# Held rotary swaps, earlier weight loads, and a last output tile in narrower pieces in a hybrid attention layer

## The chip, the cores and the metric

The kernel runs on one core of a Trainium2 chip. The metric is the time of one execution on the device in microseconds (us), taken as the median over runs. The engines are PE (matmul; its weight loads are listed as PEld), DVE (vector), ACT (activation and copies), POOL (general) and SP, which here only issues DMAs. Every engine works through its own instructions in the order in which the program lists them, and waits where an operand isn't ready.

## The reference

One decoder layer on x of 2048 rows by 1024 columns. Two groups of attention heads share one input projection; each branch is gated, and both go through one output projection, a root-mean-square norm and a gated residual:

```python
h = rms_norm(x, g_pre) * (1 + scale) + shift              # scale, shift, gate from silu(c) @ w_ada + b_ada
qa, ka, va, fa, za, qb, kb, vb, zb = split(h @ w_in)
oa = forgetting_attention(qa, ka, va, fa + b_fgate)       # FoX: 8 heads of 64, causal, with a cumulative log-forget bias
oa = oa * silu(za)
qb, kb = rope(qb, positions), rope(kb, positions)         # [x1*cos - x2*sin, x2*cos + x1*sin], halves of 32 columns
ob = sliding_window_sink_attention(qb, kb, vb, sinks)     # 8 query heads, 2 key/value heads, window 128, a sink per head
ob = ob * silu(zb)
y = concatenate([oa, ob]) @ w_out
x + gate * rms_norm(y, g_post)
```

The arithmetic is in float32; the kernel splits float32 operands into a high and a low float16 part and makes three products of them.

## The kernel before

The program is one order written by hand. Time on PE is cut into units (a few matmuls each, the list `punits`); `tick()` advances a list of delayed steps, and `after(n, f)` puts step `f` on that list for the n-th tick from now. So each engine's order is set by where a step's tick falls. `events` holds, for a unit's number, the steps that stand ahead of that unit.

The stages are: start and first projections (to about 155 us), the sliding-window stage (to 416), the FoX heads 0 to 6 (to 926), head 7 with the loading and splitting of `w_out` (to 1016), sixteen output tiles of 128 rows (to 1169), and the end.

In the sliding-window stage 32 objects of class `Pair` run in turn, each for two query blocks of 128 and two heads, and between their parts PE does projection units. A pair's steps are: `scores` (PE, L852); `maxima` (DVE, L866, L869); `exps` (ACT, four at L877); in `split` the `high` half, a float16 copy on ACT (L894) and a DMA transpose on SP's queue (L895), and the `low` half, a subtraction on DVE (L899), a second transpose (L900) and then `load_now()`; and, two pairs later, `pv` (PE, L915), which needs both transposes (`ptb`), with `out_` on DVE (L921, tile `on`). Four ticks make up one pair's turn.

Two other chains run through this stage in the same engines' orders.

- The rotation of queries, `evac_rope`. ACT copies the projected columns from PSUM to `qf` (L717); four DMAs on SP's queue write them with their 32-row blocks swapped to `qs` (L719); DVE multiplies the PSUM columns by the cosine into `qc` (L722); POOL multiplies `qs` by the sine (L732); DVE adds (L733); ACT copies the sum to float16, `stb` (L734); DVE makes its low part (L726). The pairs' scores read both parts. The steps after the copy are timed from the start of the chain, at 5, 6, 7 and 8 ticks plus `turn_lag`.
- The weights of each projection: `w_load` (a DMA into `wr_...`, queued until the next `load_now()` while `banded` is set), `w_max` (DVE, L224), a round trip through DRAM on POOL's queue, `w_scale`, then `w_high` (ACT, L267) and `w_low` (DVE, L273) into `wh_...`. `leads` in `add` says how many units ahead of its projection each step stands; for the load that is 46.

In head 7 the loop over steps `s` (with `r` the step within the head) loads the parts of `w_out`, makes its scale in `w_root` from sums of squares (`wss`), and loads the rows of the first two output tiles: `Out.load` fetches the attention output `o_d` and the gate `z_d`. `turn` transposes them on PE (L1436), multiplies by the gate on DVE (L1445), takes the squares on ACT (L1448), and splits the product into `oz`. `product` then makes two halves of 512 columns in 24 matmuls each (L1472); the evacuation squares on ACT (L1480) and multiplies by `gacc` on DVE (L1481); `root` takes the reciprocal root by small DVE operations, and `store` adds the residual (L1507) and writes the tile out (L1508). The last tile is stored in two halves.

Of the kernel before, what the change touches and what calls it, by code (L numbers as in the profile page):

```python
# [10 lines left out]
F32 = mybir.dt.float32  # L11
# [29 lines left out]
def hybrid_layer(  # L41
# [47 lines left out]
    def rsqrt_mean(dst, ss, n):  # L89

        v = sm(n, "rs_v")
        V.tensor_scalar(v[:], ss, 1.0 / D, EPS, op0=ALU.mult, op1=ALU.add)
# [106 lines left out]
    kaps_seen = []  # L199
    first = ("kb", "vb", "zb0", "zb1")  # L200

    queued, banded = [], [False]

    def load_now():
        todo, queued[:] = queued[:], []
        for key, pieces in todo:
            w_load(key, pieces, SP)
# [499 lines left out]
    def evac_rope(ci, finish, pool):  # L707
        cols_ = slice(ci * CH, (ci + 1) * CH)

        def evac(ps, free):  # L710
# [4 lines left out]

            def copy():
                A.activation(qf[:], ps, AF.Copy, scale=PS_SCALE)  # L717
                for r in range(4):
                    SP.dma_start(qs[32 * r:32 * r + 32, :], qf[32 * (r ^ 1):32 * (r ^ 1) + 32, :])  # L719
# [8 lines left out]

            after(1, copy)
            after(2, cos)  # L730
            d = turn_lag[0]
            after(5 + d, lambda: G.tensor_tensor(qs[:], qs[:], sinT[:, cols_], op=ALU.mult))  # L732
            after(6 + d, lambda: V.tensor_tensor(qc[:], qc[:], qs[:], op=ALU.add))  # L733
            after(7 + d, lambda: A.activation(stg[:, 0, :], qc[:], AF.Copy))  # L734
            after(8 + d, low)

        return evac

# [95 lines left out]
    class Pair:  # L834
# [44 lines left out]
        def split(self):  # L879
# [17 lines left out]
            def low():  # L897
                for p, (hi, lo) in cuts:
                    V.tensor_tensor(lo, p, hi, op=ALU.subtract)  # L899
                SP.dma_start_transpose(self.ptt[:, 1, 0:self.nt, :], part[1][:, 0:n])  # L900
# [26 lines left out]

    pkeys, punits = [], []  # L930
# [231 lines left out]
    def w_square(m):  # L1162
# [3 lines left out]
        if m < 32:  # L1166
            wsq[m] = wsp.tile([P, 2 * P], F32, tag="wsq", name="wsq")
            SP.dma_start(wsq[m][:], w_out0[m // 4 * P:(m // 4 + 1) * P, m % 4 * 2 * P:(m % 4 + 1) * 2 * P])

    def w_root():  # L1170
        wsum = sm(1, "w_mx2")
        V.tensor_reduce(wsum[:], wss[:], axis=AX.X, op=ALU.add)
        pw_ = bk[bank()][:, 0:1]
        PE.matmul(pw_, ones[:], wsum[:], start=True, stop=True)
        root_scale(wrt[:], pw_)
# [242 lines left out]
    class Out:  # L1418


        def __init__(self, t):
            self.t = t

        def load(self):
            t = self.t
            rows_ = slice(t * P, (t + 1) * P)
            self.o = Ts[0][:, t % 2, :].bitcast(F32)
            SP.dma_start(self.o, o_d[t // 4][(t % 4) * P:(t % 4 + 1) * P, :])
# [30 lines left out]
            after(lag + 2, lambda: V.scalar_tensor_tensor(lo, self.z, self.sc[:], hi, op0=ALU.mult, op1=ALU.subtract))  # L1459

        def product(self, n, k):
            cc = slice(n * CH, (n + 1) * CH)
            if k == 0:
                self.b = bank(True)
                if n == 0:
                    self.ss = sm(2, "y_ss")
                else:
                    self.x = oio["x"]()
                    SP.dma_start(self.x[:], xs[self.t * P:(self.t + 1) * P, :])
            py, b = bk[self.b][:], self.b  # L1470
            for m_, (i, j) in enumerate(((0, 0), (0, 1), (1, 0))):
                PE.matmul(py, self.hl[:, i, k, :], w_slot(8 * j + k)[:, cc],  # L1472
                          start=(k == 0 and m_ == 0), stop=(k == KT - 1 and m_ == 2))
# [3 lines left out]
            def evac():  # L1477
                if n == 0:
                    self.y = oio["y"]()
                A.activation(oio["j"][1 + n], py, AF.Square, accum_out=self.ss[:, n:n + 1])  # L1480
                V.tensor_tensor(self.y[:, cc], py, gacc[:, cc], op=ALU.mult)  # L1481
                release(b)

            after(1, evac)
            if n == 1:
                last = self.t == NB - 1
                after(2 if last else 4, self.root)
                after(2 if last else 7, self.store)

        def root(self):  # L1490
            ss = self.ss
            inv = sm(1, "w_sw")
            V.tensor_tensor(inv[:], self.sc[:], ysc[:], op=ALU.mult)
            V.reciprocal(inv[:], inv[:])
            V.tensor_tensor(ss[:, 0:1], ss[:, 0:1], ss[:, 1:2], op=ALU.add)
            V.tensor_scalar(ss[:, 0:1], ss[:, 0:1], inv[:], inv[:], op0=ALU.mult, op1=ALU.mult)  # L1496
            rst = sm(1, "y_rs")
            rsqrt_mean(rst, ss[:, 0:1], 1)
            V.tensor_tensor(rst[:], rst[:], inv[:], op=ALU.mult)
            self.rst = rst  # L1500

        def store(self):
            y, rst = self.y, self.rst
            parts = 2 if self.t == NB - 1 else 1
            for n in range(parts):
                cc = slice(n * D // parts, (n + 1) * D // parts)
                V.scalar_tensor_tensor(y[:, cc], y[:, cc], rst[:], self.x[:, cc], op0=ALU.mult, op1=ALU.add)  # L1507
# [5 lines left out]
    for t, n in [(0, 0), (1, 0), (0, 1), (1, 1)] + [(t, n) for t in range(2, NB) for n in range(2)]:  # L1513
        if n == 0 and t + 2 < NB:
            oloads[len(ounits)] = t + 2
        for q in range(KT):
# [16 lines left out]
    with tc.manual_schedule():  # L1533
# [29 lines left out]
        for s, stp_ in enumerate(steps):  # L1563
# [112 lines left out]
```

## Time and profile before

| what | value |
|---|---|
| three runs | 1177.09, 1177.81 and 1180.39 us; median 1177.81 |
| profiled execution | 1180.07 us, of which the span of the core's work is 1178.3 |
| mean granted clock of PE | 0.992 |
| PE busy | 1119.8 us, 95% of the span |
| DVE, ACT, POOL busy | 918.9, 679.1, 165.3 us |
| start and first projections | 0 to 155 us, PE busy 135.46 |
| sliding-window stage | 155 to 416 us, PE busy 247.21 |
| FoX heads 0 to 6 | 416 to 926 us, PE busy 502.64 |
| head 7 | 926 to 1016 us, PE busy 81.60 |
| output tiles | 1016 to 1169.4 us, PE busy 152.92 |
| end | 1169.4 to 1178.3 us, PE busy 0 |

Rows of single instructions read: start, duration, engine, line, operation, output<-inputs, partitions and columns, type, count; in brackets stands the idle time of the engine just before, and the instruction or DMA that ended it. Rows with "SPq" are DMAs on SP's queue, with the time that their issue took there. Rows of waits read: engine, instruction, what it waited for, total, times, longest. Rows of windows read: stretch, length, busy time and instructions of PE, PEld, DVE, ACT and POOL, then PE's granted clock, the share of time that DMA engines were busy, and GB/s.

### The profile page before, as it was taken

How to read it: one execution, taken by the hardware profiler on the slowest of the kernel's cores; microseconds unless marked ns; L12 is line 12 of the kernel's file. 1: busy time of each engine (PE TensorE's matmuls, PEld its weight loads, DVE VectorE, ACT ScalarE, POOL GpSimd, SP SyncE). 2: the span in 40 equal slices, each digit the busy share in tenths (PEclk: the TensorE clock that was granted, in tenths of full speed). 3: DMA queues.
4: the chain of work that ended last, by engine and by line, in shares of the span. 5: the costliest groups of instructions: out<-in, count | busy, mean ns of one | idle time of the engine just before them, and what ended most of it. 6: DMA issues, size and time to landing. Idle time of an engine off the chain costs nothing. (4 is left out here: it accounts for less than half of the span.)

```text
span 1178.3 us, 26992 instructions
## 1 busy us (share of the span) xinstructions
PE 1119.8 (95%) x10490; PEld 653.0 (55%) x10490; DVE 918.9 (78%) x2329; ACT 679.1 (58%) x1122; POOL 165.3 (14%) x302
## 2 busy tenths in 40 slices
PE   5899999999989999999999999999999989999996
PEld 1466656654459956555555555555555545555553
DVE  6776577888788747889888889978897886767665
ACT  4676445555556433676767667676676588323331
POOL 2011122233222211111111111102010000000000
PEclk9999999999999999999999999999999999999998
DMA  9645345687676832243223232213111254465652
GB/s 330 213 138 161 94 89 110 121 145 143 132 145 112 126 76 75 67 104 73 77 76 86 78 78 72 63 46 93 44 50 43 64 175 157 148 199 168 204 175 76
DMA packets 162452, 136.36 MB, mean 116 GB/s; under 512 B 95356, under 2 KB 139428, under 8 KB 162324
## 3 DMA queue, kind: packets, MB, share of 16 engines
q1 hardware_dynamic: 152532, 106.65, 35.6%
q0 software_dynamic: 9456, 27.72, 8.8%
q8 instruction: 82, 1.34, 0.5%
q14 instruction: 46, 0.38, 0.1%
q10 hardware_dynamic: 336, 0.26, 0.1%
HBM read 70.97 MB, written 25.18 MB: 82 GB/s over the span
## 5 line engine op out<-in xcount | busy, mean ns | idle before, releaser
L1313 ACT ACTIVATE p<-sta,lift,scl_qk 128x1024 f32<-128x1024 f32 (+2 forms) x160 | 172.0, 1075 | 95.7 <-PE sta L1309 89.9
L329 PE MATMUL bk<-hT,wh_qk 128*128 128x512 f16 x768 | 197.9, 378 | 0.6 <-DVE a_m L1262 0.6
L1472 PE MATMUL bk<-wohl,oz 128*128 128x512 f16 x768 | 172.4, 379 | 2.2 <-DVE oz L1459 1.0
L1324 DVE TENSOR_TENSOR pha<-p,pha 128x1024 f16<-128x1024 f32 (+2 forms) x160 | 169.7, 1061 | 0.0
L1321 ACT ACTIVATE pha<-p 128x1024 f16<-128x1024 f32 (+2 forms) x160 | 148.1, 926 | 31.6 <-POOL p L1317 26.8
L1262 DVE TENSOR_REDUCE a_m<-bk 128x1 f32<-128x512 f32 x192 | 129.4, 684 | 36.4 <-PE bk L1259 35.6
L1472 PEld LDWEIGHTS <-oz 128*128 128x128 f16 x768 | 74.4, 99 | 84.2 <-issue 1.8
L1334 PE MATMUL poa<-vt,pha 128*128 128x65 f16 x1088 | 116.5, 193 | 1.6 <-DVE ona L1343 1.6
L1337 PE MATMUL poa<-vt,pha 128*128 128x65 f16 x1088 | 116.0, 192 | 1.4 <-DVE pha L1324 1.4
L1336 PE MATMUL poa<-vt,pha 128*128 128x64 f16 x1088 | 116.3, 194 | 0.0
L1308 PE MATMUL sta<-T 128*128 128x512 f16 (+1 forms) x320 | 109.6, 347 | 6.3 <-ACT p L1313 6.3
L1259 PE MATMUL bk<-T 66*128 66x512 f16 (+2 forms) x320 | 110.5, 348 | 2.1 <-DVE a_m L1262 2.1
L1334 PEld LDWEIGHTS <-pha 128*128 128x128 f16 x1088 | 101.6, 97 | 16.3 <-DVE ona L1343 2.9
L329 PEld LDWEIGHTS <-wh_qk 128*128 128x128 f16 x768 | 70.2, 97 | 71.6 <-issue 2.9
L1336 PEld LDWEIGHTS <-pha 128*128 128x128 f16 x1088 | 101.0, 97 | 13.4
L1309 PE MATMUL sta<-T 69*128 69x512 f16 (+1 forms) x320 | 108.0, 348 | 0.0
L1337 PEld LDWEIGHTS <-pha 128*128 128x128 f16 x1088 | 100.8, 99 | 1.6 <-DVE pha L1324 1.6
L329 PE MATMUL bk<-hT,wh_za 128*128 128x512 f16 x384 | 99.9, 379 | 0.0
L347 PE MATMUL bk<-wh_va,hT 128*128 128x128 f16 x1536 | 95.9, 223 | 1.8 <-DVE wh_va L273 1.8
L347 PEld LDWEIGHTS <-hT 128*128 128x128 f16 x1536 | 90.6, 100 | 8.1 <-issue 5.5
L329 PE MATMUL bk<-hT,wh_zb 128*128 128x512 f16 x384 | 92.8, 384 | 2.2 <-DVE wh_zb L273 2.2
L1317 POOL TENSOR_SCALAR_AFFINE_SELECT p<-p 128x256 f32<-128x256 f32 x64 | 31.9, 499 | 416.3 <-ACT p L1313 411.5
(492 smaller groups left out, 1858.3 us busy)
## 6 DMA issues: line engine op xcount, KB each, us to landing
hT<-in_x_dram SPq DMA_DIRECT2D x20, 512.0 KB
wa<-in_w_ada_dram SPq DMA_DIRECT2D x16, 512.0 KB
T<-stq SPq DMA_DIRECT2D x128, 64.0 KB
T<-o_d SPq DMA_DIRECT2D x16, 512.0 KB
T<-z_d SPq DMA_DIRECT2D x16, 512.0 KB
z_d<-tz POOLq DMA_DIRECT2D x30, 256.0 KB, 2.9
out_dram<-hT SPq DMA_DIRECT2D x15, 512.0 KB
xt<-in_x_dram SPq DMA_DIRECT2D x12, 512.0 KB
```

The costliest lines, as they stand in the source:

```text
L329: PE.matmul(ps, whl[:, a, k, :], hT[ci][:, b, k, :], start=(k == 0 and n == 0), stop=(k == KT - 1 and n == 2))
L347: PE.matmul(ps[:, u * P:(u + 1) * P], hT[ci][:, a, k, u * P:(u + 1) * P], whl[:, b, k, :], start=(k == 0 and n == 0), stop=(k == KT - 1 an ...
L1259: PE.matmul(mx[:, :w], T[0:XM, 0, i * P:(i + 1) * P], T[0:XM, 2, pc * CH:pc * CH + w], start=True, stop=True)
L1262: V.tensor_reduce(m3[:, u, pc:pc + 1], mx[:, :w], axis=AX.X, op=ALU.max)
L1308: PE.matmul(self.st[:, o:o + w], T[:, 3, kb_], T[:, 1, qc], start=True, stop=False)
L1313: A.activation(self.p32[:, :self.w], self.st[:, :self.w], AF.Exp, scale=scl[f"qk{self.hd}"][:], bias=lift[:])
L1321: A.activation(self.ph[:, 0, :self.w], self.p32[:, :self.w], AF.Copy)
L1324: V.tensor_tensor(self.ph[:, 1, :self.w], self.p32[:, :self.w], self.ph[:, 0, :self.w], op=ALU.subtract)
L1334: PE.matmul(po[:, u, :], ph[:, 0, pq], vt[:, b, hd, 0:65], start=(self.first and n == 0 and u == 0), stop=False)
L1336: PE.matmul(po[:, u, 0:64], ph[:, 0, pq], vt[:, b, hd, 65:VW], start=False, stop=False)
L1337: PE.matmul(po[:, u, :], ph[:, 1, pq], vt[:, b, hd, 0:65], start=False, stop=(self.last and n == len(self.blocks) - 1))
L1472: PE.matmul(py, self.hl[:, i, k, :], w_slot(8 * j + k)[:, cc], start=(k == 0 and m_ == 0), stop=(k == KT - 1 and m_ == 2))
```

## The change

It has four parts.

1. While `banded` is set, the four swap DMAs of a rotation are put on a list, `swaps`, and issued by the next `load_now`, that is behind a pair's second transpose. The steps after them are timed from there: POOL's product 4 ticks later, DVE's add 5, ACT's copy 6, the low part 7. When swaps were issued, weight loads that are queued wait for the next pair's call.
2. The loads of weights after the first stage stand 64 units ahead of their projection (58 for `qk0`) instead of 46.
3. In head 7, the gate rows of the first two output tiles are loaded at steps 1 and 2, ahead of the attention rows at 4 and 6; every output tile loads its gate first. The last sum over `wss` for `w_root` is taken at step 134 instead of at 136.
4. The last output tile is made in pieces of 512, 384 and 128 columns, 24 matmuls each. Its factor `inv` is multiplied in at the evacuation, what can be had without the last 128 columns is computed ahead, and the second half is stored from ACT's queue.

```diff
@@ load_now, evac_rope
+    def load_now(must=True):
+        todo, swaps[:] = swaps[:], []
+        for f in todo:
+            f()
+        if todo and not must:
+            return
...
             def copy():
                 A.activation(qf[:], ps, AF.Copy, scale=PS_SCALE)
+                if banded[0]:
+                    swaps.append(lambda: (swap(), rest(4)))
+                else:
+                    swap()
+                    rest(4 + turn_lag[0])
+
+            def swap():
                 for r in range(4):
                     SP.dma_start(qs[32 * r:32 * r + 32, :], qf[32 * (r ^ 1):32 * (r ^ 1) + 32, :])
+
+            def rest(d):
+                after(d, lambda: G.tensor_tensor(qs[:], qs[:], sinT[:, cols_], op=ALU.mult))
+                after(d + 1, lambda: V.tensor_tensor(qc[:], qc[:], qs[:], op=ALU.add))
+                after(d + 2, lambda: A.activation(stg[:, 0, :], qc[:], AF.Copy))
+                after(d + 3, low)
...
@@ Pair.low
-                load_now()
+                load_now(False)
@@ add
+            if at > N_PRO and (key == "qk0" or key[:2] not in ("qk", "za")):
+                leads = (58 if key == "qk0" else 64,) + leads[1:]
@@ the loop of head 7
+            if hd == 7 and r in (1, 2):
+                outs[r - 1].load_z()
             if hd == 7 and r in (4, 6):
-                outs[r // 2 - 2].load()
+                outs[r // 2 - 2].load_o()
...
+            if s == 134:
+                w_sum()
             if s == 136:
                 w_root()
@@ Out
+            self.last = t == NB - 1
+            self.cuts = (0, CH, CH + 3 * P, D) if self.last else (0, CH, D)
...
+                A.activation(oio["j"][1 + n % 2][:, :cc.stop - cc.start], py, AF.Square, accum_out=self.ss[:, n:n + 1])
+                if self.last:
+                    if n == 0:
+                        self.unscale()
+                    V.scalar_tensor_tensor(self.y[:, cc], py, self.inv[:], gacc[:, cc], op0=ALU.mult, op1=ALU.mult)
+                    if n == 1:
+                        self.part()
+                else:
+                    V.tensor_tensor(self.y[:, cc], py, gacc[:, cc], op=ALU.mult)
...
+        def part(self):
+            ss = self.ss
+            self.sq = sm(1, "w_pw")
+            V.tensor_scalar(self.sq[:], self.inv[:], self.inv[:], 1.0 / D, op0=ALU.mult, op1=ALU.mult)
+            V.tensor_tensor(ss[:, 0:1], ss[:, 0:1], ss[:, 1:2], op=ALU.add)
+            V.tensor_scalar(ss[:, 3:4], ss[:, 0:1], self.sq[:], EPS, op0=ALU.mult, op1=ALU.add)
...
+            if self.last:
+                rsqrt_mean(rst, ss[:, 2:3], 1, self.sq[:], ss[:, 3:4])
...
-                SP.dma_start(os_[self.t * P:(self.t + 1) * P, cc], y[:, cc])
+                e.dma_start(os_[self.t * P:(self.t + 1) * P, cc], y[:, cc])
```

What this moves, on three engines' orders (line numbers are those of each kernel; the lines after the change are some 5 to 50 higher). First SP's queue at pairs 3 to 6: `sp` is a pair's high or low part on its way through a transpose into `ptb`, `qs<-qf` are the four swaps. Before:

```order
L895 DMA_TRANSPOSE ptb<-sp_1939 128x8x128
L900 DMA_TRANSPOSE ptb<-sp_1940 128x8x128
L217 DMA wr_zb_2459<-in_w_in_dram 128x8x128
L895 DMA_TRANSPOSE ptb<-sp_1941 128x8x128
L719 DMA qs<-qf 32x512 x4
L900 DMA_TRANSPOSE ptb<-sp_1939 128x8x128
L895 DMA_TRANSPOSE ptb<-sp_1940 128x8x128
L900 DMA_TRANSPOSE ptb<-sp_1941 128x8x128
L217 DMA wr_qb_2736<-in_w_in_dram 128x8x128
L895 DMA_TRANSPOSE ptb<-sp_1939 128x8x128
L719 DMA qs<-qf 32x512 x4
L900 DMA_TRANSPOSE ptb<-sp_1940 128x8x128
```

After, at the same pairs:

```order
L908 DMA_TRANSPOSE ptb<-sp_1939 128x8x128
L913 DMA_TRANSPOSE ptb<-sp_1940 128x8x128
L731 DMA qs<-qf 32x512 x4
L908 DMA_TRANSPOSE ptb<-sp_1941 128x8x128
L913 DMA_TRANSPOSE ptb<-sp_1939 128x8x128
L731 DMA qs<-qf 32x512 x4
L908 DMA_TRANSPOSE ptb<-sp_1940 128x8x128
L913 DMA_TRANSPOSE ptb<-sp_1941 128x8x128
L222 DMA wr_qb_2736<-in_w_in_dram 128x8x128
L908 DMA_TRANSPOSE ptb<-sp_1939 128x8x128
L913 DMA_TRANSPOSE ptb<-sp_1940 128x8x128
L731 DMA qs<-qf 32x512 x4
```

No swap stands between a pair's two transposes any more (before, it did at pairs 4, 6, 21 and 23), and the load of `wr_zb`, which stood behind pair 3, is gone from here: it now stands behind pair 2. The other ten of the fourteen groups of swaps move back by about one pair.

Second, ACT from pair 9's copy of the high half to pair 10's (`sm__3134` and the first `sp` are pair 9's, `sm__3240` or `sm__3241` pair 10's; `stb<-qc` is a rotation's float16 copy). Before:

```order
L894 ACTIVATE sp_1939<-sm__3134 128x1024
L734 ACTIVATE stb<-qc 128x512
L267 ACTIVATE wh_qb_3258<-wr_qb_2736,w_sw 128x1024
L717 ACTIVATE qf<-bk_138 128x512
L877 ACTIVATE sm__3240,b_rs<-sm__3240,b_nb 128x257 x4
L894 ACTIVATE sp_1941<-sm__3240 128x1024
```

After:

```order
L907 ACTIVATE sp_1939<-sm__3134 128x1024
L272 ACTIVATE wh_qb_3259<-wr_qb_2736,w_sw 128x1024
L736 ACTIVATE stb<-qc 128x512
L722 ACTIVATE qf<-bk_138 128x512
L890 ACTIVATE sm__3241,b_rs<-sm__3241,b_nb 128x257 x4
L907 ACTIVATE sp_1941<-sm__3241 128x1024
```

The copy has moved by one row here, but what it waits for has moved further. On DVE, from pair 10's last maximum to its subtraction, before (the add stood ahead of pair 9's subtraction):

```order
L866 ISA sm__3240,b_m<-pss,bmask,snk,scl_qb_2398 128x256
L866 ISA b_m 128x1
L869 TENSOR_SCALAR b_nb<-b_m 128x2
L726 TENSOR_TENSOR stb<-qc,stb 128x512
L921 TENSOR_TENSOR on<-pob,b_ri 128x256
L273 SCALAR_TENSOR_TENSOR wh_qb_3258<-wr_qb_2736,w_sw,wh_qb_3258 128x512
L722 SCALAR_TENSOR_TENSOR qc<-bk_138,cosT 128x512
L273 SCALAR_TENSOR_TENSOR wh_qb_3258<-wr_qb_2736,w_sw,wh_qb_3258 128x512
L899 TENSOR_TENSOR sp_1939<-sm__3240,sp_1941 128x1024
```

After:

```order
L879 ISA sm__3241,b_m<-pss,bmask,snk,scl_qb_2395 128x256
L879 ISA b_m 128x1
L882 TENSOR_SCALAR b_nb<-b_m 128x2
L735 TENSOR_TENSOR qc<-qc,qs 128x512
L934 TENSOR_TENSOR on<-pob,b_ri 128x256
L278 SCALAR_TENSOR_TENSOR wh_qb_3259<-wr_qb_2736,w_sw,wh_qb_3259 128x512
L744 TENSOR_TENSOR stb<-qc,stb 128x512
L740 SCALAR_TENSOR_TENSOR qc<-bk_138,cosT 128x512
L278 SCALAR_TENSOR_TENSOR wh_qb_3259<-wr_qb_2736,w_sw,wh_qb_3259 128x512
L912 TENSOR_TENSOR sp_1939<-sm__3241,sp_1941 128x1024
```

The add `qc<-qc,qs` now stands behind pair 10's maxima, so ACT's copy, and the four exps behind it, come after all of them. It is so at ten pairs where it wasn't before. PE's order is the same in both kernels but for the last tile.

Third, DVE from the last tile's last evacuation to the final multiply. Before, the rows from the evacuation to the reciprocal root's first one:

```order
L1481 TENSOR_TENSOR hT_110<-bk_6364,gacc 128x512
L1493 TENSOR_TENSOR w_sw<-w_pw,ysc 128x1
L1494 RECIPROCAL w_sw<-w_sw 128x1
L1495 TENSOR_TENSOR y_ss<-y_ss 128x1
L1496 TENSOR_SCALAR y_ss<-y_ss,w_sw 128x1
L92 TENSOR_SCALAR rs_v<-y_ss 128x1
```

After, with the rows that were moved ahead of it:

```order
L1511 SCALAR_TENSOR_TENSOR hT_110<-bk_6364,w_sw,gacc 128x384
L1531 TENSOR_SCALAR w_pw<-w_sw 128x1
L1532 TENSOR_TENSOR y_ss<-y_ss 128x1
L1533 TENSOR_SCALAR y_ss<-y_ss,w_pw 128x1
L1511 SCALAR_TENSOR_TENSOR hT_110<-bk_139,w_sw,gacc 128x128
L92 TENSOR_SCALAR rs_v<-y_ss,w_pw 128x1
```

Nothing stands between the last evacuation and the root's first operation any more; before, four operations did.

More of the change, by code (lines that the diff above doesn't have):

```diff
@@ L200, in hybrid_layer @@
     first = ("kb", "vb", "zb0", "zb1")
-    queued, banded = [], [False]
-    def load_now():
+    queued, swaps, banded = [], [], [False]
+    def load_now(must=True):
[4 more added lines that the diff above has]
+            return
         todo, queued[:] = queued[:], []
@@ L730, in evac @@
             after(2, cos)
[L731 to L735, printed above, removed]
         return evac
@@ L926, in pv @@
             after(1, out_)
-    pkeys, punits = [], []
+    pkeys, punits, N_PRO = [], [], 10 ** 6
     def add(key, us):
@@ L1168, in w_square, with w_sum @@
             SP.dma_start(wsq[m][:], w_out0[m // 4 * P:(m // 4 + 1) * P, m % 4 * 2 * P:(m % 4 + 1) * 2 * P])
+    def w_sum():
+        wsq["sum"] = sm(1, "w_mx2")
+        V.tensor_reduce(wsq["sum"][:], wss[:], axis=AX.X, op=ALU.add)
     def w_root():
-        wsum = sm(1, "w_mx2")
-        V.tensor_reduce(wsum[:], wss[:], axis=AX.X, op=ALU.add)
+        wsum = wsq.pop("sum")
         pw_ = bk[bank()][:, 0:1]
@@ L1482, in evac, with unscale @@
                 release(b)
             after(1, evac)
[L1485 to L1488, printed above, removed]
+            if n == len(self.cuts) - 2:
+                after(2 if self.last else 4, self.root)
+                after(2 if self.last else 7, self.store)
+        def unscale(self):
+            self.inv = sm(1, "w_sw")
+            V.tensor_tensor(self.inv[:], self.sc[:], ysc[:], op=ALU.mult)
+            V.reciprocal(self.inv[:], self.inv[:])
@@ L1503, in store @@
             y, rst = self.y, self.rst
-            parts = 2 if self.t == NB - 1 else 1
-            for n in range(parts):
-                cc = slice(n * D // parts, (n + 1) * D // parts)
+            for n, e in enumerate((SP, A) if self.last else (SP,)):
+                cc = slice(n * CH, (n + 1) * CH) if self.last else slice(0, D)
                 V.scalar_tensor_tensor(y[:, cc], y[:, cc], rst[:], self.x[:, cc], op0=ALU.mult, op1=ALU.add)
-                SP.dma_start(os_[self.t * P:(self.t + 1) * P, cc], y[:, cc])
+                e.dma_start(os_[self.t * P:(self.t + 1) * P, cc], y[:, cc])
     outs = [Out(t) for t in range(NB)]
     ounits, oloads = [], {}
-    for t, n in [(0, 0), (1, 0), (0, 1), (1, 1)] + [(t, n) for t in range(2, NB) for n in range(2)]:
+    for t, n in [(0, 0), (1, 0), (0, 1), (1, 1)] + [(t, n) for t in range(2, NB) for n in range(len(outs[t].cuts) - 1)]:
         if n == 0 and t + 2 < NB:
```

37 lines of the change are left out of this document (20 added, 17 removed).

## The prediction

> **What bounds the kernel now.** I read the page's busy times first, then the windows by stage, then what the PE waited for in the sliding-window stage, and last the queue of the SP engine and the single instructions at each stall.
>
> ```profile
> span 1178.3 us, 26992 instructions
> PE 1119.8 (95%) x10490; PEld 653.0 (55%) x10490; DVE 918.9 (78%) x2329; ACT 679.1 (58%) x1122; POOL 165.3 (14%) x302
> ...
> 155.00:416.00 261.00, 247.21 (x3015) 167.24 (x3012) 209.20 (x601) 139.58 (x354) 70.23 (x140) 0.98 0.66 128
> 926.00:1016.00 90.00, 81.60 (x846) 48.27 (x846) 70.59 (x144) 62.80 (x83) 7.50 (x14) 1.00 0.44 136
> ```
>
> PE is busy for 95% of the span, so time can come only from stretches in which PE stands still, runs at a lower clock, or is already done. The windows (length, then busy time of PE, weight loads, DVE, ACT and POOL, then the granted clock) show two such stages: the sliding-window stage, 261.00 us with 247.21 busy and a clock of 0.98, and the last attention head, 90.00 us with 81.60 busy. The third place is the end, after PE's last matmul. The change touches these three alone.
>
> In the sliding-window stage PE waited for this (total, times, longest):
>
> ```profile
> PE pob L915 <- DMA ptb<-sp: 7.2, 3, 3.7
> PE bk L329 <- DVE wh_zb L273: 2.2, 1, 2.2
> PE pob L915 <- DVE on L921: 2.1, 3, 0.8
> PE bk L347 <- DVE wh_va L273: 1.8, 2, 1.3
> ...
> 208.20 0.81 PE L915 MATMUL pob<-vb,ptb 128*128 128x64 f16 x22 [3.69 <-DMA ptb<-sp]
> 280.65 3.98 PE L329 MATMUL bk<-hT,wh_zb 128*128 128x512 f16 x10 [2.17 <-DVE wh_zb L273]
> 352.54 1.13 PE L915 MATMUL pob<-vb,ptb 128*128 128x64 f16 x22 [2.14 <-DMA ptb<-sp]
> ...
> 209.50:212.90 3.40, 3.40 (x33) 3.40 (x32) 2.79 (x11) 2.35 (x8) 0.75 (x1) 0.50 0.69 191
> ...
> 352.85:356.25 3.40, 3.40 (x45) 3.40 (x41) 3.16 (x8) 0.47 (x1) 1.78 (x4) 0.50 0.63 115
> 964.90:968.30 3.40, 2.98 (x39) 2.30 (x39) 2.68 (x7) 3.40 (x5) 0.00 (x0) 1.00 0.85 240
> ```
>
> Behind each of the three stalls of over 2 us stand 3.40 us at a granted clock of 0.50 (the first and the last of the three are shown, 209.50 and 352.85): such a stretch costs another 3.40 x 0.50 = 1.7 us, 5.1 us together, on top of the stalls. It doesn't always come: after a stall of 2.60 us in the last head (its row is below) the window at 964.90 shows 1.00. The Trainium skill (TensorE: Matmul & The Clock Gate, Part 1) says that the clock falls only after at least one whole idle window of about 3.4 us. By that rule only the stall of 3.69 us could be followed by the slow stretch, 1.7 us instead of 5.1 would hang on the stalls, and the most that the stage could gain (18.0 us below) would be 3.4 less; the trace differs, with 0.50 after 2.14 us too, and the measurement decides.
>
> **1. Swaps held until a pair's second transpose is issued.** The stall of 3.69 us comes from SP's queue (issue, time, kind):
>
> ```profile
> 198.11 1.25 SPq L895 DMA_TRANSPOSE ptb<-sp  x1
> 199.58 3.29 SPq L719 DMA_DIRECT2D qs<-qf  x4
> 202.98 1.26 SPq L900 DMA_TRANSPOSE ptb<-sp  x1
> ...
> 330.42 2.42 SPq L719 DMA_DIRECT2D qs<-qf  x4
> ```
>
> Four swap DMAs stand between the two transposes of pair 4 and hold the second for 3.29 us; at pairs 21 and 23 they take 2.42. With the swaps behind, the three waits of 7.2 us lose 3.29 + 2.42 + 2.42, bounded by each wait's own length (3.69, 2.14, and 7.2 less these two, 1.4): 3.3 + 1.4 + 2.1 = 6.8 us, and two of the three slow stretches go too. Gross: 6.8 + 3.4 = 10.2 us.
>
> The price is on the other side of the swap. The add (DVE) and its float16 copy (ACT) now come a pair's turn later. In ten more pairs than before the copy stands directly ahead of the four exps on ACT, and must wait for the add, which stands behind the maxima on DVE; the exps no longer overlap the maxima. The trace has both kinds of pair:
>
> ```profile
> 204.57 2.23 DVE L899 TENSOR_TENSOR sp<-sm__2589,sp 128x1024 f16<-128x1024 f32 x1 [1.98 <-ACT sp L894]
> 209.82 0.69 DVE L733 TENSOR_TENSOR qc<-qc,qs 128x512 f32<-128x512 f32 x1
> 214.27 1.23 DVE L899 TENSOR_TENSOR sp<-sm__2742,sp 128x1024 f16<-128x1024 f32 x1 [1.41 <-ACT sp L894]
> ...
> 237.02 0.69 DVE L733 TENSOR_TENSOR qc<-qc,qs 128x512 f32<-128x512 f32 x1 [0.80 <-POOL qs L732]
> 237.63 1.22 DVE L899 TENSOR_TENSOR sp<-sm__3134,sp 128x1024 f16<-128x1024 f32 x1
> 244.10 1.22 DVE L899 TENSOR_TENSOR sp<-sm__3240,sp 128x1024 f16<-128x1024 f32 x1
> ```
>
> The L899 subtraction closes each pair's loop over DVE and ACT. From end to end the pair with the add ahead of the exps takes 215.50 - 206.80 = 8.7 us, one without it 245.32 - 238.85 = 6.5: 2.2 us longer. Against that, the pair before no longer holds the add and its wait for POOL, 0.69 + 0.80 = 1.5 us, which shortens it where its subtraction doesn't wait for ACT anyway (about half of the 32 pairs do, next fence). Between 0.75 and 1.5 I take 1.1 back. So the loop grows by 10 x (2.2 - 1.1) = 11 us; with nothing returned 22.
>
> **2. Weight loads issued 58 or 64 units ahead instead of 46.** DVE waits for weights in its own order, in the midst of that same loop:
>
> ```profile
> DVE sp L899 <- ACT sp L894: 17.3, 16, 2.4
> DVE wmx L224 <- DMA wr_qb<-in_w_in_dram: 5.9, 2, 4.6
> DVE wmx L224 <- DMA wr_zb<-in_w_in_dram: 5.4, 2, 2.8
> DVE wmx L224 <- DMA wr_qk<-in_w_in_dram: 5.0, 1, 5.0
> DVE wmx L224 <- DMA wr_va<-in_w_in_dram: 3.8, 2, 3.4
> ```
>
> That is 20.1 us. The loads go out one or two pairs earlier, and one pair lasts about 7 us (between the two kinds above), against a longest wait of 5.0, so I let all of them go; between 0 (they queue at another place) and 20.1. On PE this also removes the weight stalls (2.2 + 1.8 us) and the third slow stretch, 1.7: gross 5.7 us. A load that meets the swaps is held for a further pair; where that happens to a load that was moved by one pair only, its wait stays. The loads' packets move no faster and no slower than before; their neighbours on SP are the transposes, and I cost that at nothing as long as a load follows a pair's second transpose.
>
> **1 and 2 together.** Gross, PE could gain 10.2 + 5.7 = 15.9 us, and 18.0 if the 2.1 us of waits for `on` went as well. But PE and the loop of DVE and ACT run against each other: PE already waits for `on` at three places, so there PE can't come earlier than the loop. The loop's own gain is 20.1 - 11 = 9.1 us. I take this as the stage's gain: 9.1, between -1.9 (20.1 - 22, nothing returned) and +18.0.
>
> **3. The last head.**
>
> ```profile
> 926.96 0.38 PE L1174 MATMUL bk<-w_mx,ones 128*128 128x1 f32 x2 [0.87 <-DVE w_mx L1172]
> 958.78 1.04 PE L1436 MATMUL bk<-ident,T 128*128 128x128 f32 x8
> 961.24 1.29 DVE L1445 TENSOR_TENSOR T<-bk,T 128x512 f32<-128x512 f32 x2 [3.85 <-DMA T<-z_d]
> 962.57 1.06 ACT L1448 ACTIVATE hT<-T 128x1024 bf16<-128x1024 f32 x1 [2.58 <-DVE T L1445]
> 964.86 0.38 PE L1308 MATMUL sta<-T 128*128 128x512 f16 x1 [2.60 <-ACT p L1313]
> ```
>
> The sum of w_out's squares is taken two steps sooner, so the 0.87 us wait at 926.96 goes: -0.8, between 0 and 0.9. The gate rows are the chain of the second stall: DVE waits for `z_d` until 961.24, ACT's L1448 follows, behind it on ACT the scores' `p`, and PE stands 2.60 us. With z loaded some steps sooner, DVE needs only the first four of the eight transposes, at 958.78 + 0.52 = 959.3, and the chain moves up by 1.9 us: -1.8, between 0 (another load is late) and -2.6. Later tiles load z ahead of o on SP, so an o queues behind a z that waits for its buffer; for tile 2 this is covered by the 20 us or so that the head still runs, and if that cover went it would show as a stall of some us in the output stage, which is solid now.
>
> **4. The last tile.** PE's last matmul ends at 1169.33 (8.58 us for 39, 0.22 each).
>
> ```profile
> 1160.75 8.58 PE L1472 MATMUL bk<-wohl,oz 128*128 128x512 f16 x39
> 1169.43 0.60 ACT L1480 ACTIVATE hT<-bk 128x512 bf16<-128x512 f32 x1 [4.49 <-PE bk L1472]
> 1170.15 0.69 DVE L1481 TENSOR_TENSOR hT<-bk,gacc 128x512 f32<-128x512 f32 x1 [3.30 <-ACT hT L1480]
> 1171.51 0.15 DVE L92 TENSOR_SCALAR rs_v<-y_ss 128x1 f32<-128x1 f32 x1
> 1173.67 1.42 DVE L1507 SCALAR_TENSOR_TENSOR hT<-hT,y_rs 128x512 f32<-128x512 f32 x2
> ...
> 165.80 5.41 PE L347 MATMUL bk<-wh_va,hT 128*128 128x128 f16 x94 [1.33 <-DVE wh_va L273]
> ```
>
> From there to the final multiply 4.34 us pass. The four small operations before rs_v (1170.76 to 1171.51, 0.75) leave the path, the last one (0.19) too, and square and eviction shrink to 128 columns: 0.69 to about 0.2 on DVE and 0.3 less on ACT, both estimates by width. Sum 1.7; the pointer operands of rs_v may give 0.1 back. On PE, 24 matmuls of 512 become 24 of 384 and 24 of 128: with 0.058 us at 128 columns (5.41 / 94) and 0.22 at 512, a straight line gives 0.166 at 384, so 24 x 0.004 = 0.1 more. The store from ACT's queue instead of SP's second I leave at 0, between -0.3 and +0.5. Net -1.3. The Trainium skill (TensorE: Matmul & The Clock Gate, Part 2: Back-to-back issue gap) gives about 81 ns as the sustained spacing of 128-column matmuls that each load weights; by it PE would lose 24 x 0.023 = 0.6 us more and this term would be -0.7. The row of 0.058 us, of such matmuls here, decides for the smaller loss.
>
> **Sum.** 9.1 + 0.8 + 1.8 + 1.3 = 13.0 us. The profiled execution took 1180.07 (span 1178.3), 2.26 above the median 1177.81 of the three runs; 1180.07 - 13.0 = 1167.1, and against the median 1164.8. I say 1165.
>
> **The rivals.**
> - *The late rope chain becomes the bound* (slower). Nothing of the 2.2 us is returned, so the stage's loop loses 1.9; and for the first swaps held, the low part of the rotated queries lands directly ahead of the scores that read it, so PE stalls at two scores for, as an estimate, the 2.2 us by which a pair's loop grows, with a slow stretch each: 2 x (2.2 + 1.7) = 7.8. With the 3.9 us of parts 3 and 4: 1177.8 + 1.9 + 7.8 - 3.9 = 1184. For it: the pair of 8.7 us is in the trace. Against: the waits of 20.1 us lie in the same loop. It decides from the point where the ten longer pairs cost more than 20.1 + 3.9 us.
> - *The gain of the swaps is eaten*: the waits for transposes turn into waits for `on`, and the stage gives 0 to 2 us: 1177.8 - 3.9 - 1 = 1173.
> - *All stalls go* (the added wait lies beside other work): 18.0 + 3.9 = 21.9, 1156.
>
> **How the numbers follow.** The sum as forecast (stage -5 to -14) 0.60, eaten 0.18, all stalls 0.13, slower 0.09. The forecast's own range is 1160 to 1170. For 8 in 10 the range reaches to 1158, into the full gain, and to 1174.5, past the eaten one. A change under 0.3%, 3.5 us, can't be told from none here. Faster: 0.60 + 0.13 + half of the eaten case 0.08 = 0.81; same 0.11; slower 0.08.
>
> **What would show it.** Right: no wait of PE for `ptb` in the stage over 0.8 us, no wait of DVE's L224-line maximum for `wr_` loads, clock 0.50 nowhere between 155 and 416; in the last head the stall at 926.96 gone and that at 964.86 under 1 us; from PE's end to the final multiply under 3.0 us. Wrong: new waits of PE's scores for the stored rope rows, waits for `on` well over 2.1 us in all, or loads that are still late because SP holds them behind the swaps.

## The result, and the profile after

| | before | changed |
|---|---|---|
| median of runs | 1177.45 us (four runs, 1176.82 to 1180.39) | 1166.95 us (four runs, 1165.61 to 1168.00) |
| ratio | | 0.9905, 95% interval 0.9884 to 0.9927 |
| profiled execution, its span | 1180.07, 1178.3 | 1165.92, 1164.2 |

The forecast was 1165.0 in 1158.0 to 1174.5, so the time lies 2 us from it. The changed kernel is 10.5 us faster in the medians; the two profiled executions differ by 14.1, since the one before ran 2.6 us above its median and the changed one 1.0 below. The page, the windows at the stages' new bounds, and PE's waits in the sliding-window stage after the change:

```profile
PE 1116.3 (96%) x10514; PEld 652.8 (56%) x10514; DVE 915.9 (79%) x2330; ACT 677.9 (58%) x1124; POOL 166.0 (14%) x302
...
155.00:405.00 250.00, 242.86 (x2995) 164.32 (x2994) 203.93 (x598) 137.32 (x353) 71.13 (x140) 0.99 0.65 131
915.00:1003.00 88.00, 82.29 (x862) 48.80 (x859) 70.34 (x144) 63.94 (x84) 7.52 (x14) 1.00 0.43 136
...
PE pob L928 <- DVE on L934: 3.0, 3, 2.1
PE pob L928 <- DMA ptb<-sp: 2.2, 3, 1.1
PE bk L334 <- DVE wh_zb L278: 1.0, 1, 1.0
PE bk L334 <- DVE wh_qb L278: 0.9, 1, 0.9
```

Waits for transposes fell from 7.2 to 2.2 us and those for weights from 4.0 to 1.9, while `on` rose from 2.1 to 3.0. To say where the 14.1 us lie I use four events that both programs have: the start of PE's matmul on `nn` and `triu` ahead of the stage, its first wait for `vt` when the FoX heads begin (start after that wait), its matmul for w_out's scale, and the end of its last matmul. The first two, before and then after:

```profile
146.64 0.38 PE L802 MATMUL bk<-nn,triu 128*128 128x128 f32 x2
416.60 0.30 PE L1208 MATMUL bk<-identh,cst 128*69 128x128 f16 x2 [1.06 <-DVE vt L356]
...
146.16 0.38 PE L815 MATMUL bk<-nn,triu 128*128 128x128 f32 x2
406.80 0.30 PE L1226 MATMUL bk<-identh,cst 128*69 128x128 f16 x2 [1.06 <-DVE vt L361]
```

| stretch | before | changed | difference |
|---|---|---|---|
| to the `nn` matmul | 146.64 | 146.16 | -0.5 |
| sliding-window stage, to the `vt` wait | 269.96 | 260.64 | -9.3 |
| FoX heads 0 to 6, with the wait for w_out's sum | 510.36 | 509.33 | -1.0 |
| last head and output tiles, to PE's end | 242.37 | 240.51 | -1.9 |
| end | 8.97 | 7.56 | -1.4 |

The terms of the prediction were 9.1, 0.8, 1.8 and 1.3. That they match is partly luck, as these two executions lie 3.6 us further apart than the medians, and says little yet of why; the prediction had set the stage's 9.1 as load waits won less pairs made longer, and this is what the experiments take apart.

In the pair loop on DVE, the rows to set beside those of pairs 9 and 10 before (the subtraction that closes pairs 8, 9 and 10, and the moved add; other rows between them are left out):

```profile
225.16 1.21 DVE L912 TENSOR_TENSOR sp<-sm__3029,sp 128x256 f16<-128x256 f32 x2 [1.25 <-ACT sp L907]
231.20 1.23 DVE L912 TENSOR_TENSOR sp<-sm__3134,sp 128x1024 f16<-128x1024 f32 x1 [0.42 <-ACT sp L907]
235.69 0.69 DVE L735 TENSOR_TENSOR qc<-qc,qs 128x512 f32<-128x512 f32 x1
240.62 1.22 DVE L912 TENSOR_TENSOR sp<-sm__3241,sp 128x1024 f16<-128x1024 f32 x1 [1.38 <-ACT sp L907]
```

From pair 9's subtraction to pair 10's it is now 9.42 us where it was 6.47. One place shows what such a pair can lead to. Pair 22 is one of the ten whose copy now stands ahead of the exps; pair 23 had its copy there before the change too. First the subtractions of pairs 21, 22 and 23 before, then the same after, with ACT's copy of pair 23, PE behind them, and the clock:

```profile
328.96 1.22 DVE L899 TENSOR_TENSOR sp<-sm__4381,sp 128x1024 f16<-128x1024 f32 x1
335.41 1.55 DVE L899 TENSOR_TENSOR sp<-sm__4495,sp 128x1024 f16<-128x1024 f32 x1 [0.65 <-ACT sp L894]
344.37 1.23 DVE L899 TENSOR_TENSOR sp<-sm__4594,sp 128x1024 f16<-128x1024 f32 x1 [2.37 <-ACT sp L894]
...
319.72 1.23 DVE L912 TENSOR_TENSOR sp<-sm__4381,sp 128x1024 f16<-128x1024 f32 x1 [1.02 <-DMA ptb<-sp]
329.87 1.23 DVE L912 TENSOR_TENSOR sp<-sm__4492,sp 128x1024 f16<-128x1024 f32 x1 [1.49 <-ACT sp L907]
338.50 1.23 DVE L912 TENSOR_TENSOR sp<-sm__4594,sp 128x1024 f16<-128x1024 f32 x1 [2.37 <-ACT sp L907]
...
334.78 0.63 ACT L736 ACTIVATE stb<-qc 128x512 f16<-128x512 f32 x1 [4.37 <-DVE qc L735]
...
344.10 1.00 PE L928 MATMUL pob<-vb,ptb 128*128 128x64 f16 x24 [2.06 <-DVE on L934]
...
344.80:348.20 3.40, 3.40 (x38) 3.40 (x36) 3.28 (x9) 0.00 (x0) 2.24 (x5) 0.52 0.66 127
```

Pair 23 is as long as before, 8.63 us for 8.96, and ACT stands 4.37 us there with four exps behind the copy `stb`. But pair 22 ahead of it takes 10.15 us where it took 6.45. With two long pairs in a row, PE some us later waits 2.06 us for `on` and runs on at a clock of 0.52. It is the only slow stretch left in the stage, of three.

In the last head, and at the end:

```profile
948.50 1.29 DVE L1472 TENSOR_TENSOR T<-bk,T 128x512 f32<-128x512 f32 x2 [2.03 <-PE bk L1463]
...
1156.74 0.28 ACT L1507 ACTIVATE hT<-bk 128x128 bf16<-128x128 f32 x1 [0.76 <-PE bk L1499]
1157.14 0.35 DVE L1511 SCALAR_TENSOR_TENSOR hT<-bk,w_sw,gacc 128x128 f32<-128x128 f32 x1
1157.41 0.27 DVE L92 TENSOR_SCALAR rs_v<-y_ss,w_pw 128x1 f32<-128x1 f32 x1
1159.49 1.42 DVE L1553 SCALAR_TENSOR_TENSOR hT<-hT,y_rs 128x512 f32<-128x512 f32 x2
```

The gate multiply now waits for PE's transposes, not for a DMA. PE ends at 1156.64, and 2.85 us later the final multiply starts, 4.34 before.

### The profile page after: what moved, and what is told of

It is laid out like the page before. It is cut to its first block, busy times and chain, and to the rows that moved or that the text cites. A ratio compares the mean times of both kernels' runs of the same rounds, so it can differ in the third digit from the quotient of the medians.

```text
span 1164.2 us, 27013 instructions
## 1 busy us (share of the span) xinstructions
PE 1116.3 (96%) x10514; PEld 652.8 (56%) x10514; DVE 915.9 (79%) x2330; ACT 677.9 (58%) x1124; POOL 166.0 (14%) x302
## 5 line engine op out<-in xcount | busy, mean ns | idle before, releaser
L1499 PE MATMUL bk<-wohl,oz 128*128 128x512 f16 (+2 forms) x792 | 172.5, 372 | 2.2 <-DVE oz L1486 1.0
```

## The experiments

The theory on record was that the loop over DVE and ACT limits the stage: earlier loads shorten it, held swaps lengthen it. The first rival was that PE's stalls add up and each part has its own share. The third column is the stage's length by the two events above, in the profiled execution (before 269.96, changed 260.64).

| run | median, us | stage | ratio to before, 95% interval |
|---|---|---|---|
| e1, held swaps alone | 1196.51 | 286.47 | 1.0148, 1.0128 to 1.0167 |
| e2, earlier loads alone | 1165.00 | 253.95 | 0.9869, 0.9849 to 0.9889 |
| e3, last head and tile alone | 1175.46 | 269.36 | 0.9960, 0.9946 to 0.9975 |
| e4, all, chain a tick sooner | 1181.33 | 276.24 | 1.0013, 1.0003 to 1.0024 |
| e5, all but the held swaps | 1159.38 | 254.07 | 0.9838, 0.9825 to 0.9851 |
| e6, swaps held only between transposes | 1155.93 | 250.64 | 0.9811, 0.9798 to 0.9825 |
| e7, all, copy behind the exps | 1155.33 | 250.48 | 0.9807, 0.9793 to 0.9820 |
| e8, all, swaps at once, chain late | 1166.48 | 261.84 | 0.9902, 0.9888 to 0.9916 |
| e9, e7 with the old end | 1156.89 | 250.60 | 0.9804, 0.9785 to 0.9823 |
| e10, e7 with the old last head | 1157.34 | 250.66 | 0.9806, 0.9788 to 0.9825 |
| e11, e7 with both stores on SP | 1155.71 | 250.62 | 0.9791, 0.9772 to 0.9810 |
| e12, e7 with late loads | 1177.00 | 272.15 | 0.9973, 0.9963 to 0.9983 |

The median of before, run beside them, was 1179.43 for e1 to e4, 1177.87 for e5 to e8 and 1180.64 for e9 to e12. The last four are set against e7 by their profiles first, since small differences of medians from different chips carry that shift.

**e1, the held swaps alone.** The kernel before with the edits to `load_now`, `evac_rope` and `Pair.low`, nothing else.

> Only part 1, the swaps held; weight loads, last head and last tile as before. Theory (the loop over DVE and ACT limits the stage): without the earlier loads the loop keeps its 20.1 us of load waits and grows by about 11 us, so PE wins the transposes and loses at the waits for `on` and at the weights: 0 to +6 us against before, about 1180. Rival (stalls add up, each part has its own share): the swaps bring 10.2 of the gross 15.9 us, so about -6 us, 1171.5.

Measured: 17.1 us slower, nearly three times the worst that the theory gave; the rival is out. Waits of PE, DVE and ACT in the stage (some left out):

```profile
PE pob L928 <- DVE on L934: 21.1, 7, 7.3
...
PE pss L865 <- ACT stb L736: 1.5, 1, 1.5
...
DVE wmx L229 <- DMA wr_zb<-in_w_in_dram: 12.4, 2, 6.9
DVE wmx L229 <- DMA wr_va<-in_w_in_dram: 6.6, 2, 6.4
DVE wmx L229 <- DMA wr_qb<-in_w_in_dram: 5.2, 2, 4.7
DVE wmx L229 <- DMA wr_qk<-in_w_in_dram: 3.7, 1, 3.7
...
ACT stb L736 <- DVE qc L735: 74.3, 15, 10.4
```

The transposes' waits are nearly gone (1.3 us), and in their place stand 21.1 us for `on`. The load waits on DVE have grown from 20.1 to 27.9 us: when swaps were issued at a pair's end, queued loads wait for a later call, and at 46 units that is too late. The waits that grew are those for `wr_zb` and `wr_va`, whose loads now stand later on SP's queue; those for `wr_qb` and `wr_qk` did not.

**e2, the earlier loads alone.**

```diff
+            if at > N_PRO and (key == "qk0" or key[:2] not in ("qk", "za")):
+                leads = (58 if key == "qk0" else 64,) + leads[1:]
```

> Only part 2, the weight loads issued sooner. Theory: the loop shortens by up to 20 us, but PE still stands at the three transposes (7.2 us, two slow stretches), so it wins the weight stalls and their slow stretch, 5.7 us, and the 2.1 us of `on`: -5 to -7 us, about 1171.5. Rival (a load wait on DVE is mostly hidden from PE, only the 2.2 us stall counts): -2 to -4 us, about 1174.5.

Measured: 14.4 us faster, as much as the whole change or more (10.5 in the medians, 14.1 between the profiled executions). Neither figure held: DVE has no wait for a load left, and PE's waits for transposes went from 7.2 to 3.1 us although no swap had moved.

```profile
PE pob L915 <- DMA ptb<-sp: 3.1, 2, 1.9
PE bk L1210 <- DVE vt L356: 1.1, 1, 1.1
PE bk L329 <- DVE wh_qb L273: 0.3, 1, 0.3
```

So most of those stalls were the loop's lateness, seen at the point where PE met it, and the swap in between was only the last thing in the queue. The stage is 16.0 us shorter. In the last head, which this run leaves as it was, PE lost 1.9 us of that again (244.23 for 242.37 from w_out's scale to PE's end, with a stall of 3.21 us where it was 2.60).

**e3, last head and last tile alone.** Parts 3 and 4 on the kernel before.

> Only parts 3 and 4, last head and last tile; the sliding-window stage as before. Theory: as the two traces stand from 416 us of before on, -1.0 -1.9 -1.4 = -4.3 us, about 1173. Rival (what PE wins in the last head is given back as loads of w_out or rows come late): only the end's 1.4 us, 1176.

Measured: 4.0 us faster, the theory's 4.3 within the interval.

**e4, the chain a tick sooner.**

```diff
-                    swaps.append(lambda: (swap(), rest(4)))
+                    swaps.append(lambda: (swap(), rest(3)))
```

> The changed kernel with one number altered: after held swaps are issued, POOL's product comes 3 ticks later instead of 4, and the add, the float16 copy and the low part follow one tick sooner each, so that the add stands ahead of a pair's subtraction and the copy is no longer directly ahead of the next four exps. Theory (ten longer pairs cost the loop about 11 us): PE's waits for `on` go, and part of the 7.1 us of stalls left in the stage: 4 to 8 us faster than the changed kernel, about 1160. Rival (the longer pairs lie beside other work; the loop was never the limit): within 1.5 us of the changed kernel, 1166; or slower, by the add waiting for POOL ahead of the subtraction.

Measured: as slow as before the change, 1.9 us over it; by the ratios 12.7 us slower than the changed kernel, and 15.6 in the stage. The expectation had the wrong sign, and the rival's last clause is what happened:

```profile
DVE qc L735 <- POOL qs L734: 45.5, 13, 6.2
DVE sp L912 <- ACT sp L907: 7.4, 8, 1.7
```

The add now stands ahead of the pair's subtraction, and POOL's product, which waits for the swaps, isn't there: DVE stands 45.5 us in 13 places. With all swaps held, a chain one tick sooner only moves the wait from ACT to DVE.

**e5, no swap held.** Parts 2, 3 and 4.

> Parts 2, 3 and 4 without part 1 (swaps issued as before the change). Theory (the held swaps lengthen the loop and cost more than the transposes' waits are worth): the earlier loads' 14.4 and the 4.0 us of last head and tile add up, 18 us faster than before, 6 to 7 faster than the changed kernel. Rival (the held swaps cost only where loads are late, as when they were held alone): as the changed kernel, 11 to 12 faster than before.

Measured: 18.5 us faster than before, as the theory said. Against the changed kernel the stage is 6.6 us shorter, so the held swaps as written cost 6.6 us beside early loads. PE still waits 3.3 us for transposes.

**e6, swaps held only between a pair's two transposes.** A flag is set when `high` has issued its transpose and cleared in `low`; a rotation's swaps are held only while it is set, otherwise issued at once.

```diff
-                if banded[0]:
+                if mid[0]:
                     swaps.append(lambda: (swap(), rest(4)))
```

> The changed kernel, with swaps held only when they would fall between a pair's two transposes; all others are issued at once, with their chain timed as before the change. Theory: the ten rotations whose chain came later are back in their places, and the two transposes still waited for (3.1 us when only the loads were moved) are free: 18 to 21 us faster than before. Rival (holding costs by the swaps' place behind the second transpose, not by the chain's later ticks): no better than with no swap held, 18 or less.

Measured: 21.9 us faster than before, just past the upper end of the theory. The waits for transposes are 0.3 us in all; moving the four groups of swaps that were in the way, and leaving the other ten, wins the 3.4 us that e5 leaves. Against the changed kernel, which also holds the other ten with their chains, the stage is 10.0 us shorter.

**e7, the copy behind the exps.** For the twelve held rotations behind the first two, whose result the next scores need. Four of the twelve copies (pairs 6, 8, 23 and 25) stood ahead of the exps before the change too.

```diff
-                    swaps.append(lambda: (swap(), rest(4)))
+                    swaps.append(lambda: (swap(), rest(5 if nrot[0] > 8 else 4)))
```

> The changed kernel, with the chain one tick later still for all rotations but the first two held: the float16 copy then stands behind the four exps on ACT, not ahead of them. Theory (the price of part 1 is the exps waiting behind the copy): most of the 6 us that part 1 costs comes back, 3 to 6 us faster than the changed kernel, 15 to 17 faster than before. Rival (the price is the lateness of the whole chain, of its buffers and of the scores that read it): slower than the changed kernel, by 2 us or more.

Measured: 22.5 us faster than before, about 11 faster than the changed kernel and more than the theory's 6: the price of the copy's place was larger than the 6.6 us by which holding lost against not holding, since the held swaps also win the transposes. PE's waits in the stage, its window, and ACT's rows at pair 23 (the last three exps left out):

```profile
PE bk L1228 <- DVE vt L361: 1.1, 1, 1.1
PE bk L1279 <- DVE a_m L1282: 1.0, 1, 1.0
PE pss L867 <- DVE stb L746: 0.3, 1, 0.3
...
155.00:395.00 240.00, 239.67 (x3008) 162.89 (x3007) 203.97 (x597) 139.19 (x353) 70.61 (x140) 1.00 0.71 137
...
323.87 0.51 ACT L892 ACTIVATE sm__4593<-sm__4593,b_nb 128x257 f32<-128x257 f32 x1 [4.09 <-DVE b_nb L884]
...
325.99 0.61 ACT L738 ACTIVATE stb<-qc 128x512 f16<-128x512 f32 x1
326.51 1.04 ACT L909 ACTIVATE sp<-sm__4593 128x1024 f16<-128x1024 f32 x1
```

PE is busy for 239.67 of 240 us at full clock (the waits for `vt` and `a_m` belong to the FoX heads). The exps wait for the maxima alone, and the copy follows them. The whole chain is a tick later here, but SP's queue is the changed kernel's, and DVE's add still stands between a pair's maxima and its subtraction; what leaves the path from maxima to subtraction is the copy. As PE has nothing left to win in e6 or e7, the 10.0 and 10.2 us by which their stages are shorter are what PE could gain, and the loop may have gained more.

**e8, only the chain late.** Swaps at once, the rest of the chain as in the changed kernel.

```diff
-                    swaps.append(lambda: (swap(), rest(4)))
+                    swap()
+                    swaps.append(lambda: rest(4))
```

> The changed kernel with the swap DMAs issued at once, as before the change, but the rest of the chain still timed from a pair's second transpose. Theory (the copy ahead of the exps is the price): within 2 us of the changed kernel, 10 to 13 faster than before; the transposes' waits are back, about 3 us. Rival (the price is the swap DMAs' later place, with POOL, the add and the `qf` buffer waiting for them): 16 or more faster than before.

Measured: 11.4 us faster than before, as the changed kernel. The swap DMAs' place on SP is not the price, beyond the 3.5 us by which PE's waits for transposes are longer here (5.7 for 2.2 us); ACT's wait is there, 64.9 us for 53.6 in the changed kernel:

```profile
ACT stb L737 <- DVE qc L736: 64.9, 15, 6.2
...
PE pob L929 <- DMA ptb<-sp: 5.7, 4, 3.9
```

**e9, the old end on e7.** Part 4 undone.

> The kernel of e7 (copy behind the exps) with part 4 undone: last tile in two pieces of 512 columns and the long root. Theory (the end is a chain after PE's last matmul, of which the profile shows 1.4 us less): 1.2 to 1.6 us slower than e7, 20.9 to 21.3 faster than before. Rival (the narrower pieces cost PE what the chain wins): within 0.5 us of e7.

Measured: from PE's end to the span's end 9.01 us against 7.57 in e7, so 1.4 as expected; the medians differ by 1.6. From w_out's scale to PE's end it is 240.46 against 240.50: the narrower pieces cost PE 0.04 us.

**e10, the old last head on e7.** Part 3 undone.

> The kernel of e7 with part 3 undone: gate rows loaded with the attention rows, w_out's sum taken in w_root. Theory (two stalls of PE, 0.9 and 1.9 us): 2.4 to 2.8 us slower than e7. Rival (what is won there is partly lost to other waits in the same head): 1 to 1.5 us slower.

Measured: 2.0 us in the medians, and 1.7 in the two stretches that it touches, between theory and rival. The wait for w_out's sum is back with 0.88 us (510.38 against 509.36 from the `vt` wait to it, 1.0), and behind it PE needs 241.19 against 240.50, 0.7 us: the late gate rows cost less here than the 1.9 of the first comparison, as PE's wait for `p` is 1.8 in all and not 3.0.

**e11, both stores on SP.**

```diff
-            for n, e in enumerate((SP, A) if self.last else (SP,)):
+            for n, e in enumerate((SP, SP) if self.last else (SP,)):
```

> The kernel of e7 with both halves of the last tile stored from SP's queue. Theory (the second store has its data 0.7 us after the first, and SP is free by then): within 0.4 us of e7. Rival (two queues let the second store start sooner): 0.5 us or more slower.

Measured: 0.4 us in the medians, 7.5 against 7.57 us after PE's end. The second queue brings nothing that these runs can tell.

**e12, late loads on e7.** `leads` at 46 again.

> The kernel of e7 with part 2 undone: weight loads 46 units ahead again. Theory (the load waits on DVE, about 20 us, are in the same loop and cost PE 14 to 16 us whatever the swaps do): 10 to 16 us slower than e7. Rival (the loads were late only for a loop that the copy ahead of the exps had made long): 0 to 5 us slower.

Measured: 21.7 us slower than e7 in the medians, and 21.7 in the stage, more than the theory's 16. The load waits on DVE are 12.5, 7.6, 5.2 and 4.9 us, 30.2 in all: held swaps make late loads later, as in e1.

```profile
DVE wmx L229 <- DMA wr_zb<-in_w_in_dram: 12.5, 2, 6.9
...
DVE wmx L229 <- DMA wr_va<-in_w_in_dram: 7.6, 2, 7.1
...
PE pob L930 <- DVE on L936: 12.6, 4, 5.3
```

## Why the prediction was right, and where it was not

- **The stage, 9.1 us: right in size, and right in kind for two of its terms.** It was set as 20.1 of load waits won less 11 for longer pairs, with nothing for the transposes, since the loop was to be the limit. Measured on the stage's length: earlier loads alone 16.0 (e2), freed transposes 3.4 more (e5 to e6), the ten longer pairs -10.0 (e6 to the changed kernel), 9.4 together, against 9.3 between the two profiles. The longer pairs were nearly right; the loads were 4 us too high, the transposes 3.4 too low, and that these two cancelled is luck.
- **The longer pair, 2.2 less 1.1.** Pairs 9 and 10 show 9.42 us for 6.47, 2.95 longer, and pair 9 is 231.20 - 225.16 = 6.04 for 7.03, 1.0 returned. So this couple costs 1.95 and not 1.1. Ten like it would be 19.5, and the ten cost PE 10.0; it follows that about half fell where PE wasn't waiting for the loop. That last part is worked out, not shown place by place.
- **The gross shares were wrong.** The prediction gave the swaps 10.2 us on PE and the loads 5.7. Moving the loads alone took the transposes' waits from 7.2 to 3.1 (e2); a wait put down to a transpose was mostly the loop being late. What the swaps in the way really cost is the 3.4 us between e5 and e6. The most that the stage could gain, 18.0 in the prediction, was too low as well: in e7 it is 19.5 us shorter than before.
- **A load behind held swaps, costed at "its wait stays".** At the old lead the waits grew from 20.1 to 27.9 and 30.2 us (e1, e12). In the changed kernel it is covered by the 64 units: no wait for a load is left on DVE.
- **The slower rival** named the right mechanism, the late chain as the bound. It came true in kind for the swaps alone (e1), but at another place: 21.1 us of waits for `on`, and 1.8 at the scores where the rival had set 7.8 with its slow stretches. The early loads kept it from deciding. All stalls gone, the third rival, was priced at 1156 for the change as it stood: e7 and e6, which free the loop, reach 1155.33 and 1155.93.
- **Signs named beforehand.** PE's longest wait for `ptb` is 1.1 us, not under 0.8; in the last head the stall at 926.96 is gone and that at 964.86 down to 0.8, both right; no wait of DVE for a load, right; a clock of 0.5 remains once, behind a wait for `on` of 2.06 us that the forecast didn't have; 2.85 us from PE's end to the final multiply, right.
- **Last head.** The sum of squares gave 1.0 (0.8 forecast). The gate rows gave 1.9 between the two traces (1.8 forecast), but 0.7 in e10. Against the 240.5 us from w_out's scale to PE's end that every run with part 3 shows, the old order took 240.92 in e1, 241.19 in e10, 242.37 before and 244.23 in e2. So the gate rows are worth 0.4 to 3.7 us, past the forecast's range of 0 to 2.6; what sets the size from run to run isn't shown, and that 1.9 met 1.8 is luck.
- **The end, 1.3.** 1.4 in the trace and in e9. PE's own price for the narrower pieces is 0.04 us by e9, 0.1 forecast. The Trainium skill (TensorE: Matmul & The Clock Gate, Part 2: Back-to-back issue gap) would have given 0.6 more, by the prediction's estimate; no such loss is there.

## What to carry to other kernels

Where engines run through their instructions in a fixed order, look for the loop that several of them close together, and price a moved instruction by what stands behind it there: the float16 copy of 0.6 us, moved at twelve rotations from ahead of four exps to behind them, took 10.2 us off the stage, where the whole change had taken 9.3. A wait that the profile puts down to the last DMA in a queue may only be the place where a late loop is met, so undo each part alone before believing its share. And where a delay is added to one user of a queue, count what else is flushed behind it: held swaps cost 17 us or won 3 to 4, by the lead of the loads and the ticks of their chain.

## What the runs showed of the hardware

A slow stretch of PE's clock follows a stall in some cases only. From 130 us on, one was there with each of the twelve stalls of 2.73 us or more in all fourteen traces. Of the seven between 2.0 and 2.7 it was there behind 2.05 (e1), 2.06 (changed), 2.14 and 2.17 (before), and not behind 2.05 (e5), 2.60 (before, last head) and 2.67 (e1). So the length alone doesn't decide.

The traces show what does. Up to PE's last matmul, all changes of the granted clock within a trace lie whole multiples of 3.413 us apart: the slow stretches before start at 209.49, 281.17 and 352.85, each 71.68 = 21 x 3.413 behind the one ahead. On this grid, count how long PE stood still in each window of 3.413 us. Of the windows at full clock from 130 us on, all sixteen with 2.05 us or more of idling were followed by one at 0.50, and none with 2.00 us or less. Four windows, three of them with the one behind it (length, PE's busy time, ..., clock as the third number from the end): the one ahead of 352.85 before; the one with 2.05 us idle (e1); one that was just not enough (e4, 2.00 us idle, and the window behind it still at 1.00); and the stall of 2.60 us, which a border of the grid at 963.84 cuts into 1.57 and 1.02 us:

```profile
349.43:352.84 3.41, 1.27 (x18) 0.70 (x16) 3.29 (x12) 0.83 (x3) 1.62 (x3) 1.00 0.78 154
...
364.78:368.19 3.41, 1.36 (x32) 1.08 (x31) 3.34 (x12) 2.47 (x10) 0.60 (x1) 1.00 0.55 118
368.21:371.60 3.39, 3.39 (x36) 3.39 (x34) 3.27 (x10) 0.00 (x0) 2.54 (x5) 0.50 0.74 154
...
300.09:303.50 3.41, 1.41 (x7) 0.45 (x5) 2.74 (x6) 0.63 (x1) 0.89 (x3) 1.00 0.07 14
303.50:306.91 3.41, 1.18 (x14) 0.70 (x15) 3.34 (x12) 2.86 (x9) 0.00 (x0) 1.00 0.90 193
...
960.42:963.83 3.41, 1.84 (x17) 0.86 (x15) 2.55 (x5) 1.26 (x3) 0.00 (x0) 1.00 1.00 311
963.84:967.25 3.41, 2.39 (x36) 2.00 (x36) 2.69 (x6) 3.41 (x5) 0.00 (x0) 1.00 0.68 176
```

The Trainium skill (TensorE: Matmul & The Clock Gate, Part 1) asks for an idle window of about 3.4 us; here 2.05 us of idling within one window was enough, and the measurement decides. Whether a stall of 2 to 4 us brings its 1.7 us of slow clock therefore hangs on where it falls on the grid, and the grid lies otherwise against the program in each trace: 209.49 before and 344.65 after leave remainders of 1.28 and 3.32 when divided by 3.413.

The scatter is smaller with the stalls gone: the four runs of e7 lie within 0.42 us, those of before beside them (nine) within 3.0, and the four or five each of e9, e10 and e11 within 1.2 to 1.6, against 5.3 for the seventeen of before beside those. That the stalls are the cause isn't shown.
